# Row gathers held back by a written element, and x's sums loaded later, in both expert sweeps of an encoder layer

## The chip, the cores and the metric

One core of one Trainium2 chip runs the whole kernel. The metric is the device time of one execution in microseconds, as the median of several executions. Engines are called by their names: TensorE (PE in the profile, PEld for its weight loads), VectorE (DVE), ScalarE (ACT), GpSimd (POOL) and SyncE (SP), which issues the plain DMAs.

## The reference

One layer of an encoder, float32, 256 tokens (two blocks of 128, t = 0 and 1) of width 2048. Two kinds of attention, then an expert layer called PEER, then a last normalisation:

```python
x = x + mixed @ w_out[l]                                  # attention
x = x + peer_ffn(rms_norm(x, norm2_g[l]), ...)            # PEER, below
return rms_norm(x, final_norm_g)

q = (xt @ w_query).reshape(n_tok, PEER_HEADS, 2, 128)
scores = einsum('thcd,hcnd->thcn', q, sub_keys)           # 2 x 128 keys per head
...                                                       # top 16 of 16384 pairs per token and head
u = jnp.take(expert_u, eb, axis=0)                        # rows of the chosen experts
vv = jnp.take(expert_v, eb, axis=0)
act = jax.nn.gelu(jnp.einsum('td,thkd->thk', xb, u))
return jnp.einsum('thk,thkd->td', act * gb, vv)
```

Each token chooses 8 x 16 = 128 of 16384 experts. Per expert there is one row of 2048 numbers in u and one in v.

## The kernel before

The kernel does not gather whole rows of u and v. For most columns it computes with all 16384 experts on TensorE and picks the chosen values afterwards; only the last columns are gathered row by row. There are three stages after the attention.

**First sweep (u).** For columns 0 to 1535 of u, 192 units of 128 x 1024 numbers are loaded one after the other (SP issues the loads, `load_raw`, L158). `load_split` (L165) makes two rounded parts of each: hi on ScalarE (L169) and the remainder lo on VectorE (L170). TensorE multiplies hi (L792, eight matmuls) and lo (L794, eight) with the normalised tokens; a unit can't start before its hi, nor its second half before its lo. There are three buffers each for hi and lo. The sums land in the large array A (the arena), one slice of 512 columns for every two key rows, in order of the sweep; a slice is free for other use until its turn comes.

Beside it, VectorE does two other jobs, one piece at a time between the units' lo subtractions, in an order that a planner (`advance`, L687) writes out by hand: first the searches for the top 16 (they end in unit 52), then 256 dot products for columns 1536 to 2047 (`dot`, L648). Each dot product first has GpSimd gather 128 rows, one per token, by an indirect DMA (`gather`, L643), then VectorE multiplies and sums them (L650). VectorE's order is the program's order, since the sweep stands under `manual_schedule(engines={DVE})`; GpSimd's and SP's order is found by the compiler's scheduler. Where the gathered rows go is decided by a ring (`Slots`, L74): four buffers called wm, and, when the searches are done, the eight arena slices `PAIRS` = 52 to 59, which the searches used until then. One is added after every second unit (L811), and `add` puts it in front, so that it is the next that is handed out:

```python
if selected and opened and i % 2 == 0:
    p = opened.popleft()
    spares.add(arena[:, p * 512:(p + 1) * 512], 2 * p * KA // 8 - 4)
```

A gather into such a slice waits for the last reader that the search had there; it does not wait for VectorE to come to the line above.

**Extraction.** One-hot products pick the chosen activations out of A, apply the gelu and the gates and write the weights of all experts back into A. At its end the first three units of v are already loaded and multiplied in part (L948).

**Second sweep (v).** 192 units of v's columns 0 to 1471, two of 1024 and one of 896 columns in turn, go through `load_split` and twelve matmuls each (L931 hi, L932 lo, L933 hi) into six sums. Columns 1472 to 2047 are gathered: `weigh` (L1002) gathers 128 rows into one of five row buffers and VectorE adds them, weighted, to vsum (L1004). vsum starts as x's columns 1472 to 2047, loaded from DRAM (x2d) at L1000, ahead of the loop. The 256 weighs are spread evenly over the units by `spread` (L569), from unit `WEIGH` = 5 on; here too VectorE's order is the program's. The row buffers, vsum and two further load buffers (L998) lie in memory that the extraction's tiles give up when it ends. Before the change, the gathers for the first five weighs wait for nothing but that memory.

Of the kernel before, what the change touches and what calls it, by code (L numbers as in the profile page):

```python
# [9 lines left out]
F32 = mybir.dt.float32  # L10
# [8 lines left out]
P = 128  # L19
D = 2048  # L20
S = 256
NT = 2
# [14 lines left out]
V1 = 1472  # L37
VT = D - V1
# [23 lines left out]
EARLY_HI = (62, 63, 64)  # L62
EARLY_LO = (66, 68, 70)
EARLY_PE = (67, 68, 69, 70, 70, 70)
WEIGH = 5
LAST = 3
READY = 189
W_OUT_ORDER = (4, 5, 6, 7, 0, 1, 2, 3)
# [34 lines left out]
def encoder_layer_kernel(ctx: ExitStack, tc: tile.TileContext, x, gT, w_in, gq, gk, w_out, g2,  # L103
                         w_query, sub_keys, u_head, u_tail, v_head, v_tail, gf, cst, rope, bias_a, out):
    nc = tc.nc
# [9 lines left out]
    arena = A.rearrange("p a b c -> p (a b c)")  # L115
# [5 lines left out]
    def hTs(k, part, r):  # L121
        return hTa[:, k, part, r] if k < KA else hTb[:, k - KA, part, r]
# [8 lines left out]
    def take(n, at=None):  # L131
        if at is None:
            at = pos[0]
            pos[0] += n
        assert at + n <= NK * S, at + n
        return arena[:, at:at + n]

    def mm_bank(name="mm"):
        return psm.tile([P, 512], F32, name=name, tag="mm")

    def at_bank(name="at"):
        return psa.tile([P, 512], F32, name=name, tag="at")

    def small(n, name):
        return sm.tile([P, n], F32, name=name, tag=f"s{n}", bufs=8 if n < 8 else 4)
# [19 lines left out]
    def load_split(src):  # L165
        raw = loaded.popleft() if loaded else load_raw(src)
        hi, lo = (wp.tile([P, 1024], F32R, name=s, tag=s, bufs=3)[:, :raw.shape[-1]] for s in ("hi", "lo"))
        with tc.high_priority(AHEAD):
            nc.scalar.activation(hi, raw, AF.Copy)  # L169
            nc.vector.tensor_tensor(lo, raw, hi.bitcast(F32), op=OP.subtract)  # L170
        return hi, lo
# [13 lines left out]
    def ready_sqrt():  # L185

        tc.keep_in_program_order(nc.scalar.activation(small(1, "warm"), one, AF.Sqrt))
# [102 lines left out]
    rows = Ring([take(512) for _ in range(3)])  # L290
# [206 lines left out]
    x2d = dram.tile([P, NT * D], F32, name="x2d")  # L497
# [58 lines left out]
    bg = deque()  # L556
# [83 lines left out]

    spares = Ring([arena[:, i:i + DT] for i in range(SPARE * S, NK * S, DT)])

    def gather(rows_, table, t, j):  # L643
        nc.gpsimd.indirect_dma_start(out=rows_, out_offset=None, in_=table,  # L644
                                     in_offset=bass.IndirectOffsetOnAxis(ap=experts[:, j // 32, t * 32 + j % 32:t * 32 + j % 32 + 1], axis=0))
        return rows_
# [110 lines left out]
    rows, hots, hot, one_hots = {}, {}, {}, {}  # L757

    def rows_at(q):

        bc = wp.tile([P, 1024], F32, name="bc", tag="raw", bufs=RAW)
        nc.sync.dma_start(bc, bass.AP(tensor=i1d.tensor, offset=i1d.offset + 4 * q * P, ap=[[0, P], [1, 8 * P]]))
        rows[q // 2] = bc
# [13 lines left out]
    with query:  # L777
        for i in range(units):
            if i == SPARE * KA // 8 - 2:
                del raws[1]  # L780
            hi, lo = load_split(u_head[i])

            blocks = {}
            for b in range(8):
                e, k = divmod(8 * i + b, KA)
                blocks.setdefault(e, []).append((k, slice(b * P, (b + 1) * P)))
            for e, ks in blocks.items():
                if ks[0][0] == 0:
                    ps = mm_bank("act")
                for k, c in ks:  # L790
                    h = (hTa[:, k] if k < KA else hTb[:, k - KA]).rearrange("p a t -> p (a t)")
                    nc.tensor.matmul(ps, hi[:, c], h, start=k == 0, stop=False)  # L792
                for k, c in ks:
                    nc.tensor.matmul(ps[:, :S], lo[:, c], hTs(k, 0, slice(0, S)), start=False, stop=k == KA - 1)  # L794
                if ks[-1][0] == KA - 1:
                    ended.append((i + 3, A[:, e // 2, :, e % 2], ps))
                    with tc.high_priority(FIRST):
                        nc.scalar.activation(ended[-1][1], ps[:, :S], AF.Copy)
            while ended and (ended[0][0] <= i or i == units - 1):
                _, dst, sums = ended.popleft()  # L800
                nc.vector.tensor_tensor(dst, dst, sums[:, S:], op=OP.add)
            advance()
            if not searches and not selected:
                selected = True
                for t in range(NT):
                    select_transposed(t)
                opened = deque(range(*PAIRS))

            spares.now = i + 1
            if selected and opened and i % 2 == 0:  # L810
                p = opened.popleft()  # L811
                spares.add(arena[:, p * 512:(p + 1) * 512], 2 * p * KA // 8 - 4)
            if i == READY:
                tp = at_bank("parttp")
                for t in range(NT):
                    nc.tensor.transpose(tp[:, t * P:(t + 1) * P], part[:, t], ident)
                nc.scalar.activation(partT, tp[:, :S], AF.Copy)
                tp = at_bank("roottp")
                for t in range(NT):
                    nc.tensor.matmul(tp[:, t * P:(t + 1) * P], roots[:, NT + t:NT + t + 1].to_broadcast([P, P]), ident,  # L820
                                     start=True, stop=True)
                nc.scalar.activation(rootT, tp[:, :S], AF.Copy)
            if i == units - 1:
                for q in range(0, FULL, 2):
                    rows_at(q)
                for q in range(FULL):
                    hot_at(q)()
# [108 lines left out]
    def v_unit(i):  # L936
        return v_head[i][:, :2 * VW[2]] if i % 3 == 1 else v_head[i]
# [59 lines left out]
    vp = ctx.enter_context(tc.tile_pool(name="vp", bufs=2))  # L997
    raws.append((vp, MORE))  # L998
    vsum = vp.tile([P, NT, VT], F32, name="vsum", bufs=1)
    nc.sync.dma_start(vsum, x2d.rearrange("p (t d) -> p t d", t=NT)[:, :, V1:])  # L1000

    def weigh(t, j):  # L1002
        rows_ = gather(vp.tile([P, VT], F32, name="rows", bufs=5), v_tail, t, j)
        nc.vector.scalar_tensor_tensor(vsum[:, t], rows_, wN[:, t, j:j + 1], vsum[:, t], op0=OP.mult, op1=OP.add)  # L1004

    for t in range(NT):
        bg.extend((0.6, weigh, t, j) for j in range(P))


    ssl = [small(4, "ssl") for _ in range(NT)]  # L1010
# [1 line left out]
    with tc.manual_schedule(engines={DVE}):  # L1012
        for i in range(units):
            if i in halves:
                jobs = halves.pop(i)
                for job in jobs:
                    if job[2] == 0:
                        weights_at(job[1], slice(P, S))
            else:
                jobs = v_jobs(i, *load_split(v_unit(i)))  # L1020
                for job in jobs[::2]:
                    if job[2] == 0:
                        weights_at(job[1], slice(0, S))
            if i < units - LAST:
                for job in jobs:
                    v_matmuls(*job)
            else:
                last += jobs
            if i == 3 * units // 4:
                nc.sync.dma_start(xs[:, :, :V1], x2d.rearrange("p (t d) -> p t d", t=NT)[:, :, :V1])  # L1030
                load_gain(gf)
                ready_sqrt()
            if WEIGH <= i < units - 1:
                spread(units - 7 - i)
            if i == units - 5:
                for t in range(NT):
                    nc.vector.tensor_copy(xs[:, t, V1:], vsum[:, t])
                    square_sum(t, 3, ssl[t], v_chunk)
                    gained(t, 3)


        ends = ((2, 0, 1), (0, 1, 2))
        for t in range(NT):
            for c in ends[t]:
                for job in last:
                    if job[0] == t and job[2] == c:
                        v_matmuls(*job)
        for t in range(NT):
            for n, c in enumerate(ends[t]):
                xc = xs[:, t, v_chunk(c)]  # L1050
                nc.vector.tensor_tensor(xc, xc, v_bank(t, c), op=OP.add)
                with tc.high_priority(FIRST if t else 0):
                    square_sum(t, c, ssl[t], v_chunk)
                gained(t, c, nc.vector if t or n == VC - 1 else nc.gpsimd)
                if (t, n) == (1, 0):
                    scaled(0, ssl[0], ((3, nc.scalar), (1, nc.scalar), (0, nc.scalar), (2, nc.vector)))
        with tc.high_priority(FIRST):
            scaled(1, ssl[1], ((0, nc.vector), (1, nc.scalar), (2, nc.vector), (3, nc.scalar)))
# [78 lines left out]
```

## Time and profile before

| | |
|---|---|
| median of 3 runs | 1649.62 us (1647.13 to 1651.18) |
| profiled execution: its own time | 1659.56 us |
| profiled execution: span | 1657.8 us |
| mean granted TensorE clock | 0.994 |
| busy: TensorE, VectorE, ScalarE, GpSimd | 98%, 82%, 52%, 43% |
| first sweep in the trace | about 441 to 992 us |
| second sweep in the trace | from about 1131 us |

The span runs from the first to the last instruction of the profiled execution. Busy shares are averages over the span; engines work beside each other. The TensorE clock is granted at one of two levels, 1.00 (2.4 GHz) and 0.50 (1.2 GHz). "L792" is line 792 of the kernel; in a row, what stands before `<-` is written and what stands behind it is read, x8 is a count, and a bracket tells how long the engine had been idle and what ended that. "issue" in a bracket means that the engine waited for nothing that the profile shows.

### The profile page before, as it was taken

How to read it: one execution, taken by the hardware profiler on the slowest of the kernel's cores; microseconds unless marked ns; L12 is line 12 of the kernel's file. 1: busy time of each engine (PE TensorE's matmuls, PEld its weight loads, DVE VectorE, ACT ScalarE, POOL GpSimd, SP SyncE). 2: the span in 40 equal slices, each digit the busy share in tenths (PEclk: the TensorE clock that was granted, in tenths of full speed). 3: DMA queues.
4: the chain of work that ended last, by engine and by line, in shares of the span. 5: the costliest groups of instructions: out<-in, count | busy, mean ns of one | idle time of the engine just before them, and what ended most of it. 6: DMA issues, size and time to landing. Idle time of an engine off the chain costs nothing.

```text
span 1657.8 us, 25499 instructions
## 1 busy us (share of the span) xinstructions
PE 1627.9 (98%) x8706; PEld 1408.2 (85%) x8706; DVE 1358.7 (82%) x3030; ACT 867.1 (52%) x1255; POOL 705.2 (43%) x582
## 2 busy tenths in 40 slices
PE   8999999999999999999999999998999999999997
PEld 6888888888888878888888889997888888888886
DVE  6765465569799978888888859996899999999996
ACT  6565555454444444444444449995444444444444
POOL 0000000001233367676766613334676766667670
PEclk9999999999999999999999999999999999999999
DMA  7644554566777689999999863335999999999994
GB/s 248 198 144 153 166 202 165 191 206 202 231 253 245 235 303 345 347 340 338 347 341 313 300 241 116 128 118 201 356 389 365 347 357 344 356 349 359 340 365 146
DMA packets 126162, 443.04 MB, mean 267 GB/s; under 512 B 17744, under 2 KB 18640, under 8 KB 125648
## 3 DMA queue, kind: packets, MB, share of 16 engines
q1 hardware_dynamic: 85072, 298.78, 51.7%
q0 software_dynamic: 40960, 142.64, 24.3%
q8 instruction: 68, 1.11, 0.3%
q14 instruction: 62, 0.51, 0.1%
HBM read 437.02 MB, written 4.33 MB: 266 GB/s over the span
## 4 chain that ended last, share of the span: by engine, by line
PE 94%; DVE 2%; DMA 1%; ACT 1%; issue 1%; SPq 0%; ACTq 0%; DVEq 0%
PE act L792 21%; PE act L794 11%; PE o L932 10%; PE o L933 10%; PE o L931 10%; PE pr L275 7%; PE pr L276 7%; PE pr L274 7%; PE X L846 3%; PE W L896 3%; PE o1p L852 1%; PE sc L356 1%; PE po L387 1%; DMA raw<-in_v_head_dram 1%; DVE lo L170 1%
## 5 line engine op out<-in xcount | busy, mean ns | idle before, releaser
L169 ACT ACTIVATE hi<-raw 128x1024 fp32r<-128x1024 f32 (+1 forms) x445 | 464.8, 1045 | 529.9 <-PE o L933 241.0
L170 DVE TENSOR_TENSOR lo<-raw,hi 128x1024 fp32r<-128x1024 f32 (+1 forms) x445 | 536.0, 1205 | 187.2 <-ACT hi L169 166.0
L792 PE MATMUL act<-hTa,hi 128*128 128x512 f32 x1536 | 399.3, 395 | 0.8 <-issue 0.8
L644 POOL DMA_INDIRECT rows<-in_v_tail_dram,experts x256 | 321.1, 1254 | 161.7 <-DVE vsum L1004 96.0
L644 POOL DMA_INDIRECT A<-in_u_tail_dram,experts x128 | 158.5, 1239 | 471.9 <-DVE den L636 408.6
L792 PEld LDWEIGHTS act<-hTa,hi 128*128 128x128 f32 x1536 | 272.7, 190 | 46.9 <-issue 2.2
L931 PE MATMUL o<-hi,wt 128*128 128x512 f32 (+1 forms) x768 | 294.5, 384 | 3.9 <-ACT hi L169 3.9
L932 PE MATMUL o<-lo,wt 128*128 128x512 f32 (+1 forms) x768 | 294.3, 383 | 0.5 <-DVE lo L170 0.4
L933 PE MATMUL o<-hi,wt 128*128 128x512 f32 (+1 forms) x768 | 294.0, 383 | 0.0
L794 PEld LDWEIGHTS act<-hTa,lo 128*128 128x128 f32 x1536 | 219.5, 191 | 24.5 <-issue 3.5
L644 POOL DMA_INDIRECT wm<-in_u_tail_dram,experts x128 | 168.0, 1313 | 166.7 <-DVE wm L650 122.3
L794 PE MATMUL act<-hTa,lo 128*128 128x256 f32 x1536 | 226.5, 283 | 3.0 <-issue 3.0
L1004 DVE SCALAR_TENSOR_TENSOR vsum<-rows,h2t,vsum 128x576 f32<-128x576 f32 x256 | 208.7, 815 | 10.3 <-DMA rows<-in_v_tail_dram,experts 7.7
L931 PEld LDWEIGHTS o<-hi,wt 128*128 128x128 f32 x768 | 145.0, 189 | 28.5 <-ACT hi L169 4.3
L932 PEld LDWEIGHTS o<-lo,wt 128*128 128x128 f32 x768 | 144.9, 189 | 25.5 <-DVE lo L170 1.1
L933 PEld LDWEIGHTS o<-hi,wt 128*128 128x128 f32 x768 | 144.9, 189 | 24.6 <-DVE wt L926 0.6
L274 PE MATMUL pr<-hi,hTa 128*128 128x512 f32 x408 | 164.2, 404 | 0.0
L275 PE MATMUL pr<-lo,hTa 128*128 128x512 f32 x408 | 159.9, 392 | 0.3 <-DVE lo L170 0.2
L276 PE MATMUL pr<-hi,hTa 128*128 128x512 f32 x408 | 159.5, 391 | 0.0
L169 ACT ACTIVATE hi<-A 128x1024 fp32r<-128x1024 f32 x72 | 76.6, 1065 | 76.1 <-PE act L792 36.8
L170 DVE TENSOR_TENSOR lo<-A,hi 128x1024 fp32r<-128x1024 f32 x72 | 88.3, 1227 | 27.0 <-ACT hi L169 17.3
L889 POOL TENSOR_SCALAR o<-cs,I2T,h2t 128x128 f32<-128x128 f32 x64 | 54.9, 862 | 114.5 <-DVE h2t L880 56.2
(159 smaller groups left out, 2003.4 us busy)
## 6 DMA issues: line engine op xcount, KB each, us to landing
raw<-in_v_head_dram SPq DMA_DIRECT2D x128, 512.0 KB
raw<-in_u_head_dram SPq DMA_DIRECT2D x120, 512.0 KB
raw<-in_w_in_dram SPq DMA_DIRECT2D x72, 512.0 KB
A<-in_u_head_dram SPq DMA_DIRECT2D x72, 512.0 KB
raw<-in_v_head_dram SPq DMA_DIRECT2D x64, 448.0 KB
raw<-in_w_out_dram SPq DMA_DIRECT2D x32, 512.0 KB
raw<-in_w_query_dram SPq DMA_DIRECT2D x32, 512.0 KB
bc<-i1d SPq DMA_DIRECT2D x32, 512.0 KB
```

The lines of the kernel that those rows point to most:

```text
L169: nc.scalar.activation(hi, raw, AF.Copy)
L170: nc.vector.tensor_tensor(lo, raw, hi.bitcast(F32), op=OP.subtract)
L274: nc.tensor.matmul(ps[t], xT(k, 0, r), hi[:, c], start=first, stop=False)
L275: nc.tensor.matmul(ps[t], xT(k, 0, r), lo[:, c], start=False, stop=False)
L276: nc.tensor.matmul(ps[t], xT(k, 1, r), hi[:, c], start=False, stop=last)
L644: nc.gpsimd.indirect_dma_start(out=rows_, out_offset=None, in_=table, in_offset=bass.IndirectOffsetOnAxis(ap=experts[:, j // 32, t * 32 + ...
L792: nc.tensor.matmul(ps, hi[:, c], h, start=k == 0, stop=False)
L794: nc.tensor.matmul(ps[:, :S], lo[:, c], hTs(k, 0, slice(0, S)), start=False, stop=k == KA - 1)
L931: nc.tensor.matmul(ps, w[:, 0, r], hi[:, c], start=e == 0, stop=False)
L932: nc.tensor.matmul(ps, w[:, 0, r], lo[:, c], start=False, stop=False)
L933: nc.tensor.matmul(ps, w[:, 1, r], hi[:, c], start=False, stop=e == NK - 1)
L1004: nc.vector.scalar_tensor_tensor(vsum[:, t], rows_, wN[:, t, j:j + 1], vsum[:, t], op0=OP.mult, op1=OP.add)
```

## The change

A new helper writes one column of a row buffer on VectorE. A gather into that buffer writes the same place, so it has to wait until VectorE has reached the helper's instruction in its order. In the first sweep this is done for each of the eight arena slices as it is added to the ring. In the second sweep the gathers are now called from two places: five at unit `FETCH` = 4, each with its written element, and one after every weigh, for the weigh five later, without one. The first weigh moves from unit 5 to unit 7. The load of vsum moves from ahead of the loop to unit 4, behind the five gathers.

```diff
-WEIGH = 5
+FETCH, WEIGH, ROWS = 4, 7, 5
...
+    def held(rows_):
+
+        nc.vector.memset(rows_[:, 0:1], 0.0)
...
             if selected and opened and i % 2 == 0:
                 p = opened.popleft()
+                held(arena[:, p * 512:(p + 1) * 512])
                 spares.add(arena[:, p * 512:(p + 1) * 512], 2 * p * KA // 8 - 4)
...
     vsum = vp.tile([P, NT, VT], F32, name="vsum", bufs=1)
-    nc.sync.dma_start(vsum, x2d.rearrange("p (t d) -> p t d", t=NT)[:, :, V1:])
-
-    def weigh(t, j):
-        rows_ = gather(vp.tile([P, VT], F32, name="rows", bufs=5), v_tail, t, j)
+    picks, coming = deque((t, j) for t in range(NT) for j in range(P)), deque()
+
+    def fetch(hold=False):
+        if picks:
+            t, j = picks.popleft()
+            rows_ = vp.tile([P, VT], F32, name="rows", bufs=ROWS)
+            if hold:
+                held(rows_)
+            coming.append((t, j, gather(rows_, v_tail, t, j)))
+
+    def weigh():
+        t, j, rows_ = coming.popleft()
         nc.vector.scalar_tensor_tensor(vsum[:, t], rows_, wN[:, t, j:j + 1], vsum[:, t], op0=OP.mult, op1=OP.add)
-
-    for t in range(NT):
-        bg.extend((0.6, weigh, t, j) for j in range(P))
+        fetch()
+
+    bg.extend((0.6, weigh) for _ in range(NT * P))
...
+            if i == FETCH:
+                for _ in range(ROWS):
+                    fetch(hold=True)
+                nc.sync.dma_start(vsum, x2d.rearrange("p (t d) -> p t d", t=NT)[:, :, V1:])
             if WEIGH <= i < units - 1:
                 spread(units - 7 - i)
```

## Rows read from the trace of the kernel before

**Rows 1.** The page, part 1: busy time, share of the span, instructions.

```profile
PE 1627.9 (98%) x8706; PEld 1408.2 (85%) x8706; DVE 1358.7 (82%) x3030; ACT 867.1 (52%) x1255; POOL 705.2 (43%) x582
```

**Rows 2.** What TensorE waited for, whole span: us in total, times, longest.

```profile
PE o L931 <- ACT hi L169: 3.9, 1, 3.9
PE act L794 <- issue: 3.0, 5, 0.9
...
PE o L932 <- DVE lo L170: 0.4, 1, 0.4
```

**Rows 3.** Timeline of TensorE, units 53 to 59: start, us, what, count.

```profile
596.20 1.11 PE L794 MATMUL act<-hTa,lo 128*128 128x256 f32 x8
597.14 2.00 PE L792 MATMUL act<-hTa,hi 128*128 128x512 f32 x8
...
602.75 1.09 PE L792 MATMUL act<-hTa,hi 128*128 128x512 f32 x4
...
611.36 3.62 PE L792 MATMUL act<-hTa,hi 128*128 128x512 f32 x8
...
619.42 0.87 PE L792 MATMUL act<-hTa,hi 128*128 128x512 f32 x3
```

**Rows 4.** Stretches: us, busy PE, PEld, DVE, ACT, POOL, PEclk, DMA share, GB/s.

```profile
600.00:604.00 4.00, 3.84 (x21) 2.96 (x20) 1.40 (x5) 0.40 (x1) 3.08 (x4) 1.00 1.02 404
...
700.00:800.00 100.00, 100.00 (x573) 87.78 (x573) 86.50 (x177) 46.64 (x60) 71.53 (x59) 1.00 0.97 342
...
1149.60:1156.20 6.60, 6.17 (x15) 5.02 (x16) 5.08 (x6) 2.92 (x3) 1.69 (x1) 0.51 0.58 188
...
1300.00:1600.00 300.00, 300.00 (x1371) 257.13 (x1370) 275.74 (x315) 139.73 (x154) 201.60 (x163) 1.00 0.98 352
```

**Rows 5.** Timeline of GpSimd: the first and the last of 17 gathers in a row.

```profile
585.73 1.82 POOL L644 DMA_INDIRECT A<-in_u_tail_dram,experts  x1 [0.30 <-DVE A L626]
...
608.36 0.95 POOL L644 DMA_INDIRECT wm<-in_u_tail_dram,experts  x1 [0.30 <-issue]
```

**Rows 6.** Timeline of TensorE at the start of the second sweep.

```profile
1145.35 0.39 PE L933 MATMUL o<-hi,wt 128*128 128x512 f32 x1
1149.64 0.74 PE L931 MATMUL o<-hi,wt 128*128 128x448 f32 x1 [3.91 <-ACT hi L169]
...
1156.21 0.40 PE L931 MATMUL o<-hi,wt 128*128 128x512 f32 x1
```

**Rows 7.** The chain of waits there: start, us, what.

```profile
1137.81 10.75 DMA raw<-in_v_head_dram
```

**Rows 8.** Timeline there: SP's queue, and the first and last of five gathers.

```profile
1137.14 0.62 SPq L1000 DMA_DIRECT2D vsum<-x2d  x1
1137.42 1.04 POOL L644 DMA_INDIRECT rows<-in_v_tail_dram,experts  x1 [2.37 <-ACT A L897]
1137.81 1.06 SPq L160 DMA_DIRECT2D raw<-in_v_head_dram  x2
...
1142.53 1.43 POOL L644 DMA_INDIRECT rows<-in_v_tail_dram,experts  x1 [0.30 <-issue]
```

**Rows 9.** Timeline of VectorE: the one memset of a 128 x 1 column.

```profile
0.80 0.06 DVE L195 MEMSET one<- 128x1 f32 x1 [0.80 <-PEq L1125]
```

**Rows 10.** Timeline of VectorE in unit 53: lo, then a dot product on an arena row.

```profile
592.19 1.24 DVE L170 TENSOR_TENSOR lo<-raw,hi 128x1024 fp32r<-128x1024 f32 x1
...
593.69 0.68 DVE L650 SCALAR_TENSOR_TENSOR A<-A,h2t 128x512 f32<-128x512 f32 x1
```

**Rows 11.** Timelines late in the first sweep: two gathers, and the dot products that used them.

```profile
941.62 1.16 POOL L644 DMA_INDIRECT wm<-in_u_tail_dram,experts  x1 [0.39 <-DVE wm L650]
...
946.13 0.68 DVE L650 SCALAR_TENSOR_TENSOR wm<-wm,h2t 128x512 f32<-128x512 f32 x1
...
950.02 1.16 POOL L644 DMA_INDIRECT wm<-in_u_tail_dram,experts  x1 [0.39 <-DVE wm L650]
...
955.60 0.69 DVE L650 SCALAR_TENSOR_TENSOR wm<-wm,h2t 128x512 f32<-128x512 f32 x1 [1.01 <-DMA wm<-in_u_tail_dram,experts]
```

## The prediction

> **What bounds the kernel now.** I read the busy shares first, then what TensorE waited for, then the timeline around each wait. TensorE is busy for 98% of the span [rows 1], so a microsecond counts only if TensorE stops or slows for it. In the list of its waits two lie where the change works: 3.9 us for a rounded weight tile (hi, L169), with 0.4 us for its remainder (lo, L170), at the start of the second sweep, and several short waits at L794 for "issue", that is for nothing the profile shows, in the first sweep [rows 2].
>
> The first-sweep entry is larger than the list says. A unit of that sweep is eight L792 and eight L794 matmuls. Unit 54 starts at 597.14, unit 56 at 602.75, so a unit takes 2.80 us. Unit 57 starts only at 611.36 and unit 59 at 619.42 [rows 3]. From unit 56 to unit 59 pass 16.67 us where 3 x 2.80 = 8.40 are due: **8.3 us lost**. Units 57 and 58 take 8.06 us of it instead of 5.60, since TensorE is at half its clock: the eight L792 of unit 57 take 3.62 us, those of unit 54 took 2.00. That is 2.5 us; the other 5.8 are slow dispatch inside unit 56. Just before, the DMA engines are full, 404 GB/s at a share of 1.02 [rows 4], and GpSimd has issued 17 gathers in a row, the first at 585.73, the last at 608.36 [rows 5]. They are gathers into arena rows (A) that had come free, most of them for dot products that VectorE reaches much later.
>
> The second-sweep entry: the next matmul after 1145.35 was due 0.23 us later and starts at 1149.64, a hole of 4.1 us. The 15 matmuls from there to 1156.21, 6.57 us, run at a granted clock of 0.51; 0.39 us of that are the wait for lo, and half of the rest is lost to the clock: 3.5 us. Together **7.5 us** [rows 2, 4, 6]. The chain of waits names the cause: a weight load that took 10.75 us to land [rows 7]. On SP's queue it stands directly behind vsum, x's sums (576 KB), and beside five gathers that GpSimd issues from 1137.42 to 1142.53 [rows 8]. These gathers have no hurry: VectorE uses the first after unit 5.
>
> **The second sweep after the change.** The load of vsum moves on SP's queue behind the loads up to unit 4's, so unit 4's load goes out some 0.7 us earlier and has 576 KB less in front of it. The five gathers wait on VectorE for a written element behind unit 4's lo, some 1143.7 us instead of 1137.42. Waiting on GpSimd behind them: only further gathers of the same kind. Nothing holds up VectorE: the first weigh now stands in unit 7, three units or some 8 us behind the five memsets, while a gather takes about 5 us (below). Five memsets cost 5 x 0.06 us by the one memset in the trace [rows 9], beside TensorE. 256 weighs are spread from unit 7 on instead of unit 5, some 1% more VectorE work per unit; it is busy for 275.7 of 300 us there, so that is covered [rows 4]. Bounds: nothing gained, if loads still collide, to the whole 7.5. I take 7.5, because only the collision made the landing long. Next in line would be unit 5's load, behind vsum; it is needed 2.4 us later than unit 4's.
>
> **The first sweep after the change.** Here the same trick stands in another place. From the code, worked through by hand: when the searches end, in unit 52, every second unit opens one arena row, eight in all. The ring hands out the new row first, so the **next** dot product in VectorE's order takes it. VectorE's order is fixed by hand. In the trace of before, the place of the first memset is 592.19: there the lo of unit 53 begins, and at 593.69 the dot product on an A row follows [rows 10]. So between the memset and the instruction that needs the gather there lie 1.5 us of work at most. Before, the gather had been issued 8 us or more ahead; after, it can't start before the memset.
>
> What a gather takes, from its start on GpSimd until VectorE goes on, is seen where VectorE waited for one: start 950.02, use 955.60 after 1.01 us of waiting, so 5.6 us. Shorter ones exist: one that started at 941.62 was used, without a wait, at 946.13, so it took 4.5 us or less [rows 11]; the least that any row vouches for is the 0.95 us for which GpSimd is busy [rows 5]. I take 5.0, between the two, and 0.2 us for the way from VectorE to GpSimd. A hole is then 5.2 - 1.5 = 3.7 us, eight holes 29.6 us. What catches it: VectorE's idle time, 13.5 us in 100 [rows 4], over 16 units of 2.80 us makes 6.0 us; and its lead, lo of unit 53 ready at 593.43, used by TensorE at 596.20 [rows 3, 10], 2.8 us. The rest, 29.6 - 6.0 - 2.8 = **21 us**, stops TensorE, because lo comes late. At 4.5 us a gather it is 17 us. If the held gather also queues behind one other on GpSimd (17 in 22.6 us, so 1.4 us from one to the next [rows 5]), it is 32 us. Queued behind each held gather on GpSimd are the later gathers; if they come late, later dot products wait too, which the upper bound takes in. Eight memsets are 0.5 us of VectorE. Nothing later gives TensorE time back: it is the bound in every stage after.
>
> The 8.3 us of this stage go, since the 17 gathers no longer come at once. But whether the timed runs have them is a choice. The profiled execution took 1659.56 us, the median is 1649.62, 9.94 lower, and 8.3 of that would be this stall, in which TensorE waits for nothing that is named. I take it to be of the profiled execution alone. Sum against the profiled execution: 1659.56 + 21 - 7.5 - 8.3 = 1664.8; against the median: 1649.62 + 21 - 7.5 = **1663**.
>
> **The rivals.**
> 1. **The median holds the stall too.** The burst of gathers is in the program, so every run has it; against it speaks the gap of 9.94 us. Then 1663 - 8.3 = 1655.
>  The Trainium skill, "Runtime: NRT & Kernel Launch", in its part on the launch sequence, tells of a gap of about 6.2 us between a profile's total and the reported time, whatever the kernel. By that, 3.7 of the 9.94 us would be left for the stall, and an estimate for the median would lie between the two cases; no run here shows which.
> 2. **The holes are covered: faster.** Its place is VectorE between memset and dot product. It decides when a gather is ready within 1.5 + (6.0 + 2.8) / 8 = 2.6 us of its memset; then only the second sweep changes: 1649.62 - 7.5 = 1642, or 1634 if the stall goes as well. For it: VectorE runs well ahead of TensorE later in this sweep. Against it: the gather that was waited for took 5.6 us, and one of 2.4 us is in no row.
> 3. **A shorter gather.** In the trace a gather holds GpSimd for 0.95 us at 608.36 and for 1.82 us at 585.73 [rows 5]. If all eight are of the short kind, some 0.8 us each, 6 in all, come off: 1657.
>  The Trainium skill, "SBUF — State Buffer", "Who interferes with whom", says that a VectorE instruction with two SBUF inputs holds up a GpSimd instruction that reads SBUF. By that rule a VectorE standing in a hole would let the gather through faster; the trace has both lengths, and does not settle which one a held gather gets.
> 4. **Half clock on top.** TensorE, stopped every second unit, falls to 1.2 GHz, as it did behind both losses above [rows 3, 4]. The first of these spells cost 2.5 us; four of them make 1673.
>
> **How the numbers follow.** Chances: the forecast 0.42 (1663, by its bounds, 17 and 32 us, 1659 to 1674), rival 1 0.18, rival 2 0.20, rival 3 0.10, rival 4 0.10. A difference of 0.3%, 5 us, is about what a measurement of this kernel can tell from no change. Rival 1 lies at +5, so I split it between same and slower; of rival 2 nearly all is faster. Faster 0.19, same 0.11, slower 0.70. The range reaches from rival 2's 1642 to 1676, a little over rival 4, and leaves out rival 2 with the stall gone and a gather queued behind two others.
>
> **What the profile will show.** Right: TensorE without the 3.9 us wait at the start of the second sweep and with full clock there; vsum behind unit 4's load on SP's queue; eight waits of VectorE for a gather into A, 3 to 4 us each, and TensorE waiting for lo between units 53 and 69, about 21 us. Wrong: VectorE's waits there under 1.2 us, or TensorE busy through them (rival 2); a second sweep that still waits for a load; or the burst stall still there.

## The result, and the profile after

The changed kernel takes **1679.92 us** (median of 4 runs, 1678.66 to 1681.97); the kernel before took 1650.05 us in the same set (1647.13 to 1651.18). The ratio is 1.0181, with a 95% interval of 1.0169 to 1.0193: some 30 us slower. The forecast was 1663, with a range up to 1676. Its direction was right, its size too small by 17 us, and the result lies outside the range.

The page of the changed kernel: busy shares, the chain that ended last, and the dot products on arena rows (L654; L650 before).

```profile
PE 1634.3 (97%) x8706; PEld 1412.4 (84%) x8706; DVE 1357.2 (81%) x3043; ACT 867.1 (52%) x1255; POOL 711.8 (42%) x582
...
PE 81%; issue 7%; POOL 4%; DVE 3%; DMA 3%; ACT 1%; SPq 0%; POOLq 0%; ACTq 0%; DVEq 0%
...
L654 DVE SCALAR_TENSOR_TENSOR A<-A,h2t 128x512 f32<-128x512 f32 x128 | 85.7, 684 | 42.5 <-DMA A<-in_u_tail_dram,experts 42.5
```

The shares hardly moved against [rows 1]. The last row is the finding: VectorE stood 42.5 us ahead of dot products on arena rows, all of it for gathers. Asked for VectorE's waits between 590 and 690 us, the trace has one entry:

```profile
DVE A L654 <- DMA A<-in_u_tail_dram,experts: 42.5, 8, 5.9
```

Eight waits, one for each held row, the longest 5.9 us, and no other wait at all. So VectorE sets the pace from the first hole to the last. TensorE's own waits, over the whole span:

```profile
PE act L798 <- DVE lo L170: 21.4, 9, 3.8
...
PE o L937 <- DVE lo L170: 0.4, 1, 0.4
```

The 3.9 us for hi at the start of the second sweep [rows 2] are gone, a wait of 0.4 us for lo is still there, and 21.4 us of waiting for lo in the first sweep are new. That is less than the sweep lost. Unit 48 starts at 579.94 and unit 72 at 682.00; the stretch between them, first in the kernel after, then in an execution of the kernel before that had no stall (experiment 1); columns as in [rows 4]:

```profile
579.90:682.00 102.10, 80.71 (x393) 67.54 (x391) 59.54 (x133) 33.43 (x53) 50.44 (x43) 0.88 0.64 225
```

```profile
579.90:647.80 67.90, 67.90 (x393) 59.67 (x393) 61.94 (x129) 33.42 (x53) 52.61 (x41) 1.00 0.96 346
```

The same 24 units take 102.1 instead of 67.8 us: **34.3 us lost**. TensorE idles for 21.4 of them. For the other 12.9 it is busy, but slower, with a granted clock of 0.88 on average: it fell to 0.50 six times, each time in or just behind a wait for lo. VectorE's 59.54 us of work and 42.5 us of waiting make 102.0 of the 102.1 us, so nothing but its work and its holes set the length of this stretch. The DMA share falls from 0.96 to 0.64.

One of the holes, on VectorE:

```profile
592.26 1.22 DVE L170 TENSOR_TENSOR lo<-raw,hi 128x1024 fp32r<-128x1024 f32 x1
592.28 0.06 DVE L645 MEMSET A<- 128x1 f32 x1
593.40 0.41 DVE L805 TENSOR_TENSOR A<-A,act 128x256 f32<-128x256 f32 x1
598.72 0.69 DVE L654 SCALAR_TENSOR_TENSOR A<-A,h2t 128x512 f32<-128x512 f32 x1 [4.91 <-DMA A<-in_u_tail_dram,experts]
```

And on GpSimd, around the first hold (first two rows), the third (next two) and the sixth (last two):

```profile
591.99 1.15 POOL L648 DMA_INDIRECT wm<-in_u_tail_dram,experts  x1 [1.34 <-DVE wm L654]
593.45 0.94 POOL L648 DMA_INDIRECT A<-in_u_tail_dram,experts  x1 [0.31 <-issue]
...
611.84 1.67 POOL L648 DMA_INDIRECT wm<-in_u_tail_dram,experts  x1 [0.30 <-DVE A L645]
613.82 0.95 POOL L648 DMA_INDIRECT A<-in_u_tail_dram,experts  x1 [0.31 <-issue]
...
644.00 1.67 POOL L648 DMA_INDIRECT A<-in_u_tail_dram,experts  x1 [0.30 <-DVE A L645]
645.98 0.95 POOL L648 DMA_INDIRECT A<-in_u_tail_dram,experts  x1 [0.30 <-issue]
```

The element is written at 592.28. GpSimd is then busy with another gather, and starts the held one 1.17 us later. VectorE uses its row at 598.72, 5.27 us after that start. At the third hold another gather goes first once the element is written, and the held one starts 2.3 us behind it. The sixth to eighth hold are like the third; at the sixth (element at 643.66) the gather that goes first has an arena row too, one that a dot product had just freed. Which gather a waiting dot product waited for is told by the semaphore that both name in the trace. By it, in us:

| hold | 1 | 2 | 3 | 4 | 5 | 6 | 7 | 8 | mean |
|---|---|---|---|---|---|---|---|---|---|
| element to start of the held gather | 1.17 | 1.21 | 2.32 | 1.17 | 1.21 | 2.32 | 2.32 | 2.32 | 1.76 |
| start to use of the row | 5.27 | 5.22 | 4.64 | 6.28 | 6.24 | 3.78 | 4.04 | 4.62 | 5.01 |
| VectorE's wait ahead of that use | 4.91 | 4.89 | 5.76 | 5.92 | 5.91 | 4.91 | 4.83 | 5.41 | 5.32 |

All eight held gathers kept GpSimd for 0.94 or 0.95 us.

The second sweep, SP's queue and the first of the five gathers, which answer to [rows 8]; the load behind vsum, from the chain of waits; TensorE's wait for it; and the stretch of the first 15 units, columns as in [rows 4]:

```profile
1163.72 0.62 SPq L1049 DMA_DIRECT2D vsum<-x2d  x1
...
1171.12 1.04 POOL L648 DMA_INDIRECT rows<-in_v_tail_dram,experts  x1 [9.87 <-DVE rows L645]
...
1164.38 8.16 DMA raw<-in_v_head_dram
...
1174.94 0.50 PE L937 MATMUL o<-lo,wt 128*128 128x512 f32 x1 [0.39 <-DVE lo L170]
...
1157.20:1201.30 44.10, 43.62 (x209) 36.61 (x208) 34.14 (x51) 20.10 (x25) 25.75 (x20) 1.00 0.90 313
```

vsum now stands behind four weight loads instead of three, and the gathers start 13.9 us behind the sweep's first matmul (1157.24) instead of 6.4. The first 15 units, measured from that matmul to the first one of unit 15, take 44.02 us; before they took 50.89. The granted clock is 1.00 throughout. The 0.4 us for lo is not the wait of before: that stood in unit 4, this one in unit 5, whose load is now the one behind vsum and takes 8.16 us. That is the load which the prediction named as next in line. Outside these 15 units, the two kernels agree to 0.1 us from unit 72 of the first sweep on, and to 0.3 us ahead of unit 48.

### The profile page after: what moved, and what is told of

Read it like the earlier page. It is cut to its first block, busy times and chain, and to the rows that moved or that the text cites. A ratio compares the mean times of both kernels' runs of the same rounds, so it can differ in the third digit from the quotient of the medians.

```text
span 1677.1 us, 25522 instructions
## 1 busy us (share of the span) xinstructions
PE 1634.3 (97%) x8706; PEld 1412.4 (84%) x8706; DVE 1357.2 (81%) x3043; ACT 867.1 (52%) x1255; POOL 711.8 (42%) x582
## 4 chain that ended last, share of the span: by engine, by line
PE 81%; issue 7%; POOL 4%; DVE 3%; DMA 3%; ACT 1%; SPq 0%; POOLq 0%; ACTq 0%; DVEq 0%
PE act L796 14%; PE o L937 10%; PE o L938 10%; PE o L936 10%; PE act L798 7%; PE pr L275 7%; PE pr L276 7%; PE pr L274 7%; POOL wm L648 4%; PE X L851 3%; PE W L901 3%; DMA A<-in_u_tail_dram,experts 2%; DVE lo L170 1%; PE o1p L857 1%; PE sc L356 1%
## 5 line engine op out<-in xcount | busy, mean ns | idle before, releaser
L796 PE MATMUL act<-hTa,hi 128*128 128x512 f32 x1536 | 403.5, 399 | 0.0
L648 POOL DMA_INDIRECT rows<-in_v_tail_dram,experts x256 | 328.0, 1281 | 147.7 <-DVE vsum L1017 73.2
L796 PEld LDWEIGHTS act<-hTa,hi 128*128 128x128 f32 x1536 | 276.8, 192 | 46.2
L798 PEld LDWEIGHTS act<-hTa,lo 128*128 128x128 f32 x1536 | 221.0, 193 | 45.6 <-DVE lo L170 25.2
L798 PE MATMUL act<-hTa,lo 128*128 128x256 f32 x1536 | 228.6, 286 | 21.4 <-DVE lo L170 21.4
L654 DVE SCALAR_TENSOR_TENSOR A<-A,h2t 128x512 f32<-128x512 f32 x128 | 85.7, 684 | 42.5 <-DMA A<-in_u_tail_dram,experts 42.5
```

## The experiments

My theory behind the result: held gathers, issued just ahead of their use, stop VectorE (34 us lost), and the second sweep's part brings some 7 us. Its rivals: the excess over my 21 us is a queue on GpSimd, the half clock, or the 8.3 us stall that I had taken out. The runs came in three sets, the first and the third on the same chip, the second on another. The kernel before took 1657.18 us (1649.39 to 1660.41) in the first, which held experiments 2 to 5, 1650.44 (1645.98 to 1653.19) in the second (1, 6, 7 and 8), and 1649.89 (1645.77 to 1652.79) in the third (9, 10 and 11); ratios are to the runs of the kernel before in the same set. In the table, "units 48 to 72" and "first 15 units of v" are read from the timeline of TensorE, as above.

| kernel | first sweep | second sweep | units 48 to 72 | first 15 units of v | us | ratio |
|---|---|---|---|---|---|---|
| before, first profile | plain | before | 76.1 | 50.89 | | |
| after | 8 holds | after | 102.1 | 44.02 | 1679.92 | 1.0181 |
| 1. before again | plain | before | 67.8 | 47.69 | 1648.48 | one run |
| 2. second sweep only | plain | after | 76.0 | 44.55 | 1651.64 | 0.9967 |
| 3. first sweep only | 8 holds | before | 101.9 | 45.65 | 1685.44 | 1.0176 |
| 4. new row at the back | 8 holds, last in ring | after | 72.4 | 44.18 | 1651.71 | 0.9965 |
| 5. hold ahead of the dots | 8 holds, earlier | after | 93.5 | 43.74 | 1671.29 | 1.0088 |
| 6. half held | 4 holds | after | 85.1 | 43.90 | 1662.15 | one run |
| 7. no hold at all | plain | order alone | 67.9 | 48.36 | 1649.92 | 1.0000 |
| 8. every fourth unit | plain, fewer rows | after | 69.6 | 44.81 | 1647.76 | 0.9989 |
| 9. hold without the move | plain | 5 holds alone | 69.3 | 47.11 | 1648.38 | 0.9994 |
| 10. second sweep only, again | plain | after | 68.8 | 43.58 | 1645.83 | 0.9978 |
| 11. every fourth, again | plain, fewer rows | after | 70.0 | 44.65 | 1647.61 | 0.9987 |

**Experiment 1. The kernel before, profiled again.** No edit.

> The kernel before, unchanged, profiled once more. If both losses that I read from its first profile belong to the program, units 48 to 72 of the first sweep again take about 76.1 us instead of 67.8, with 'issue' waits in units 53 to 60, and the first 60 matmuls of the second sweep again take about 50.9 us with one wait of 3 us or more for hi. If they are chance, one or both are missing: about 67.8 us, about 44 to 46 us.

Measured: 48 to 72 in 67.8 us, TensorE without a single wait there; the second sweep's first 15 units in 47.69. So the stall of the first profile is not in every execution. The hole in the second sweep is there again, but smaller; TensorE's longest wait there:

```profile
PE o L931 <- ACT hi L169: 2.0, 1, 2.0
```

**Experiments 2 and 3. The two parts apart.** Experiment 2 is the changed kernel without the first sweep's hold, experiment 3 the kernel before with it:

```diff
# experiment 2, to the kernel after
-                held(arena[:, p * 512:(p + 1) * 512])
# experiment 3, to the kernel before (with the helper)
+                held(arena[:, p * 512:(p + 1) * 512])
```

> The changed kernel without the eight memsets of the first sweep; the second sweep stays changed. My theory (the eight holds of the first sweep cost some 34 us, the second sweep gains some 7): the holds gone, VectorE has no wait for a gather into A of over 3 us, TensorE's sum of waits for lo in the first sweep goes from 21.4 us to under 2, and the time is 1650 - 7 = 1643. Rival (the new calling order of the second sweep's gathers, or the changed order that the scheduler finds, costs most of the 30 us): 1660 or more. Second rival (the loss of the first sweep that the profile of before showed is in every execution of before): the time again 1643, but with slow dispatch of TensorE after unit 55 in this trace too.

> The kernel before with the eight memsets of the first sweep added, second sweep as before. My theory: the two halves add up, so 1650 + 34 = 1684, with eight waits of VectorE for a gather into A, 42 us in all, and the 3.9 us wait of TensorE at the start of the second sweep back. Rival (the second sweep did not gain, the 30 us are all of the first sweep): 1680.

Experiment 2: ratio 0.9967 [0.9947, 0.9987], a gain, but 1651.64 us instead of the 1643 expected. Its profile suggests why: the stall is back, and in that set the kernel before took 7 us more as well. TensorE's waits:

```profile
PE act L798 <- issue: 3.7, 4, 1.7
```

Experiment 3: ratio 1.0176 [1.0141, 1.0211], 1685.44 us. It repeats the first sweep of the change: VectorE's waits from 590 to 690 us are

```profile
DVE A L654 <- DMA A<-in_u_tail_dram,experts: 42.8, 8, 5.9
```

and units 48 to 72 take 101.9 us. So the loss is in the first sweep's eight holds. The ratio makes it 23 to 35 us, with the 34 inside; the 1685.44 us meet the 1684 expected, though the profiled execution took 1680.47 and the kernel before was 7 us above its usual time in this set. The other thing it shows I had not expected: with the second sweep untouched, its first 15 units took 45.65 us, not 50.89, and the wait for hi that was to come back was 0.6 us, not 3.9.

**Experiment 4. The held row at the back of the ring.** The holds stay; only their row is used last instead of first.

```diff
-                spares.add(arena[:, p * 512:(p + 1) * 512], 2 * p * KA // 8 - 4)
+                spares.views.append((arena[:, p * 512:(p + 1) * 512], 2 * p * KA // 8 - 4))
```

> The changed kernel, holds and all, but a new row goes to the back of the ring, so that at least four dot products (some 2.4 units, 6.8 us) lie between its memset and its use. My theory (what costs is the short way from memset to use, 1.5 us of work against a gather of 6.7 us): no wait of VectorE for A of over 2 us, time 1643 as without the holds. Rival (a hold costs in itself, since GpSimd stands still behind the held gather and the later gathers come late): waits of VectorE move to wm rows, time 1660 or more.

Ratio 0.9965 [0.9949, 0.9981], the same as without holds. VectorE's waits for gathers, 590 to 690 us:

```profile
DVE A L654 <- DMA A<-in_u_tail_dram,experts: 1.8, 2, 1.5
```

42.5 us of waiting became 1.8. **It is not the written element that costs, but that the very next dot product needs its row.** The 1651.71 us, where 1643 was expected, go with that set again; its profile has a shorter stall, 4.6 us in units 60 to 64.

**Experiment 5. The element written ahead of the unit's dot products**, which also opens the rows two units later.

```diff
+            if selected and opened and i % 2 == 0:
+                held(arena[:, opened[0] * 512:(opened[0] + 1) * 512])
+                held_now = True
+            else:
+                held_now = False
             advance()
...
-            if selected and opened and i % 2 == 0:
+            if held_now:
                 p = opened.popleft()
-                held(arena[:, p * 512:(p + 1) * 512])
```

> The changed kernel with each memset of the first sweep ahead of its unit's dot products instead of behind them (the eight rows open two units later, from unit 54 on). This puts one or two dot products, 0.6 us each, between memset and use, and the held gather comes ahead of the gathers that these dot products set free. If the excess over my forecast is the queue on GpSimd (memset to start of the gather 1.3 us instead of 0.2): the gap from memset to start falls to some 0.3 us, the holes to about 3.4 us, 27 us in all, and the time to 1665. If the queue stays: holes of about 4.4 us, 1672. If the half clock makes the excess: no less than 1675.

Ratio 1.0088 [1.0053, 1.0122], 1671.29 us. VectorE's waits:

```profile
DVE A L654 <- DMA A<-in_u_tail_dram,experts: 33.0, 8, 5.3
...
DVE lo L170 <- issue: 1.5, 2, 1.2
```

The holes shrink from 42.5 to 33.0 us, 4.1 each, and the lost time from 34.3 to 93.5 - 67.8 = 25.7 (the holes and the 1.5 us of "issue", less the 8.8 of idle time and lead). From element to use pass 6.5 us on average instead of 6.8, so 1.0 of the 1.2 us by which a hole is shorter is the added work. The queue did get shorter, but not to 0.3 us: element to start on GpSimd is 1.1 us on average instead of 1.76, and start to use 5.4 instead of 5.0. The time agrees with "the queue stays", but the rows open at other moments than in the change, so this run alone does not tell the queue from the gather's length. The times read from the change do that.

**Experiment 6. Every second row held.**

```diff
-                held(arena[:, p * 512:(p + 1) * 512])
+                if p % 2 == 0:
+                    held(arena[:, p * 512:(p + 1) * 512])
```

> The change with the held element at every second opened arena row only, four instead of eight. If each hold makes its hole of 5.3 us whatever the others do, and VectorE's idle time and lead (8.8 us) are spent once, units 48 to 72 take 67.8 + 4 x 5.3 - 8.8 = 80.2 us. If the loss is simply by the hold, half of the 34.3 us of the change, 84.9 us. If the unheld rows beside them bring back the burst of gathers, up to 8 us of 'issue' waits come on top.

Units 48 to 72 take 85.1 us, where the first theory gave 80.2 and the second 84.9. VectorE's waits, and GpSimd around the second hold (element written at 607.68):

```profile
DVE A L654 <- DMA A<-in_u_tail_dram,experts: 24.9, 4, 6.9
...
DVE lo L170 <- ACT hi L169: 2.3, 2, 1.2
```

```profile
608.02 1.68 POOL L648 DMA_INDIRECT wm<-in_u_tail_dram,experts  x1 [0.30 <-DVE A L645]
610.00 0.95 POOL L648 DMA_INDIRECT wm<-in_u_tail_dram,experts  x1 [0.30 <-issue]
611.25 0.94 POOL L648 DMA_INDIRECT A<-in_u_tail_dram,experts  x1 [0.30 <-issue]
```

The holes are longer, 24.9 / 4 = 6.2 us, and this one is the longest, 6.9: two other gathers went ahead of the held one, so it started 3.6 us behind its element. With the holes as measured, 24.9 - 8.8 = 16.1 against 17.3 us lost, "each hole, less idle time and lead once" fits within 1.2; "half of the eight" fits as well, 17.2. This run doesn't part the two. No "issue" waits of TensorE came on top. What it shows is that the holes grow beside unheld gathers: over the four, element to start is 2.1 us on average, against 1.76 with eight holds, and start to use 5.6 against 5.0.

**Experiment 7. No hold anywhere, the second sweep's new order alone.**

```diff
# to the kernel of experiment 2
-                    fetch(hold=True)
+                    fetch()
```

> No held element anywhere; in the second sweep only the order is new (gathers called at unit 4 without a written element, the first weigh in unit 7, the load of x's sums behind unit 4's load). If moving the load of x's sums is what freed unit 4's load, the first 60 matmuls of the second sweep take 44 to 45 us, as in the change, and the ratio to before is that of the kernel with the second sweep's part alone, 0.997. If the five gathers beside it are the cause, they start at about 1137 us again, a wait of 2 us or more for hi is left, the 60 matmuls take 48 to 51 us, and the ratio is 1.000.

Ratio 1.0000 [0.9988, 1.0011], 48.36 us for the first 15 units. TensorE's wait, the chain of waits with the weight load behind it, and the first of the five gathers:

```profile
PE o L935 <- ACT hi L169: 2.0, 1, 2.0
...
1131.06 10.91 DMA raw<-in_v_head_dram
...
1130.29 1.04 POOL L648 DMA_INDIRECT rows<-in_v_tail_dram,experts  x1 [2.37 <-ACT A L901]
```

Called later in the program, the gathers still start at the same point of the sweep, 6.4 us behind its first matmul: what starts them is their release, not their line. Beside them a weight load takes 10.91 us, as in [rows 7]. It is unit 5's this time, the one that now stands behind vsum; so moving vsum alone passes the wait on to the next unit and brings nothing.

**Experiment 9. The five gathers held, vsum loaded ahead of the loop as before.**

```diff
# to the kernel of experiment 2
     vsum = vp.tile([P, NT, VT], F32, name="vsum", bufs=1)
+    nc.sync.dma_start(vsum, x2d.rearrange("p (t d) -> p t d", t=NT)[:, :, V1:])
...
                     fetch(hold=True)
-                nc.sync.dma_start(vsum, x2d.rearrange("p (t d) -> p t d", t=NT)[:, :, V1:])
```

> No held element in the first sweep; in the second the five gathers are held at unit 4 as in the change, but the load of x's sums is back ahead of the loop, as before. If the five gathers alone delay the load of unit 4, the first 60 matmuls of the second sweep take 44 to 45 us, no wait for hi over 1 us is left, and the ratio to before is that of the second sweep's part alone in the same call. If the load of x's sums ahead of it counts as well, they take 46 us or more, with a wait for hi of 1 us or more, and the ratio lies between that one and 1.000.

Ratio 0.9994 [0.9985, 1.0003], 47.11 us. The wait for hi is half as long, and the weight load behind vsum takes 7.84 us without gathers beside it:

```profile
PE o L935 <- ACT hi L169: 1.0, 1, 1.0
...
1131.15 7.84 DMA raw<-in_v_head_dram
```

So neither half is enough: each alone leaves a wait of 1 to 2 us and a spell of half clock (mean granted clock 0.96 over the first 15 units in both). One profile each would not show that, since the second sweep of before took anything from 45.65 to 50.89 us; the times do. The ratio of experiment 7 is 1.0000, and this kernel took 1647.21 to 1653.01 us, where that of experiment 10, with both halves, took 1644.25 to 1647.51 in the same set. With both, the load behind vsum is unit 5's, which is needed later, and the gathers come too late to hold it up; the clock stays full. The stretch in the kernel of experiment 10:

```profile
1124.80:1168.40 43.60, 43.51 (x208) 36.59 (x207) 34.01 (x51) 20.23 (x25) 25.25 (x20) 1.00 0.91 319
```

**Experiments 8, 10 and 11. Which version is best.** Experiment 10 repeats experiment 2; 8 and 11 are the same kernel with rows opened after every fourth unit:

```diff
# experiments 8 and 11, to the kernel of experiment 2
-            if selected and opened and i % 2 == 0:
+            if selected and opened and i % 4 == 0:
```

> No held element in the first sweep; an arena row is opened after every fourth unit instead of every second; the second sweep as in the change. If the 'issue' stall comes from the long run of back-to-back gathers that the freed rows allow, it shrinks to under 3 us, units 48 to 72 take 68 to 71 us, and the ratio to before is 0.992 to 0.994. If the stall comes whenever the gathers start, it stays at 8 us and the ratio is 0.997. If fewer open rows let dot products wait, TensorE waits for lo at L798 and the ratio is over 0.997.

> The second sweep's part of the change alone, once more, against more runs of before. If that part is worth 4 us, as four profiles without held gathers (45.7 to 50.9 us for the first 60 matmuls) stand to those with them (43.7 to 44.8), the ratio is 0.9976. If it is worth the 7.5 us of my prediction, 0.9955. If the earlier 0.9967 was chance, 1.000.

> The second sweep's part with arena rows opened after every fourth unit, no held element in the first sweep, once more. If spreading the rows saves the chance of an 'issue' stall, it lies 1 to 6 us under the kernel with the second sweep's part alone in the same call; if that stall is rare on this chip, the two agree within 1 us, less the 1.8 us that one short wait for lo cost in its first profile.

Experiment 10: ratio **0.9978 [0.9969, 0.9987]**, 1645.83 us, 4 us under the kernel before, as the theory of 4 us had it. It beats both kernels. Every fourth unit gave 0.9989 [0.9977, 1.0001] and 0.9987 [0.9978, 0.9996], where 0.992 to 0.994 was one expectation; the latter is 1.8 us above experiment 10 in the same set. The profile of experiment 11 has two short waits of TensorE at L798 (0.59 and 1.02 us) in units 56 to 60, that of experiment 8 one of 1.5 us for lo. So fewer open rows save nothing where the stall is absent. Whether they would avoid it stays open, since none of the profiles of the second and third sets has one.

## Why the prediction was wrong in size

The mechanisms were right; two terms of the sum were mis-sized, the queue ahead of a held gather and the second sweep's gain.

**The hole per hold, the term that failed most.** I wrote: "A hole is then 5.2 - 1.5 = 3.7 us, eight holes 29.6 us." Measured: 42.5 / 8 = 5.3 us. Two of its three parts were right: "I take 5.0, between the two" was 5.0, and the work between was 1.76 + 5.01 - 5.32 = 1.45. The step that failed is "0.2 us for the way from VectorE to GpSimd", for which I gave no row. It was 1.76: at four holds GpSimd was busy with another gather when the element was written, at the other four one more went first. Eight times 1.56 is 12.5 of the 12.9 us missing. The idle time and lead that catch part of it, 8.8, measured 42.5 - 34.3 = 8.2. The case "If the held gather also queues behind one other on GpSimd ... it is 32 us" stood in the text as a bound. It was the likely case, and its 0.2 + 1.4 us are close to the 1.76: [rows 5] shows GpSimd issuing gathers back to back in just this stretch, so a new one finds a queue.

One sign came true by luck. I had TensorE "waiting for lo between units 53 and 69, about 21 us", and it waited 21.4. But my 21 us were to be the whole loss; the loss was 34.3, and the other 12.9 us went into a slower TensorE.

The length from start to use also answers rival 3. Its condition held, all eight held gathers were of the short kind, but its 6 us did not come off: the held gather at 593.45 took GpSimd only 0.94 us, and its row was used 5.27 us after the start. A short gather on GpSimd is not an early row. The Trainium skill, "Perfetto Trace Analysis", in its section "DMA Instruction — SWDGE (GPSIMD)", says that the profiled end there is the end of writing descriptors, not of moving data; the trace agrees. The Trainium skill, "DMA: Bandwidth & Descriptors", in its section "Anatomy of one DMA — SWDGE (gpsimd) path", gives 2.0 us plus the bytes at 436 GB/s, for these 128 x 512 floats an estimate of 2.6 us; the trace differs, with 3.8 to 6.3 us from start to use among the other transfers.

**The second sweep's gain.** I wrote "I take 7.5, because only the collision made the landing long." Against its own profile the change gained 50.89 - 44.02 = 6.9 us, so the cause was read rightly. But that profile was at the bad end: the three with this part of the kernel unchanged took 50.89, 47.69 and 45.65, mean 48.1, and the eight with the second sweep of the change 43.58 to 44.81, mean 44.2. The gain is **3.9 us** on average, and experiment 10's ratio says the same. The cause was the pair, gathers and vsum (experiments 7 and 9).

**The sum, mended.** 1650.05 + 34.3 - 3.9 = 1680.4; measured 1679.92. Of the 17 us between forecast and result, 13.3 are the first sweep's and 3.6 the second's.

**The stall.** "I take it to be of the profiled execution alone" held for the set that the forecast was about: an execution without it took 1648.48 us, beside a median of 1650.05. It is not a flaw of that one profile, though. In the first set of experiments it was in the profile of experiment 2, and shorter in that of experiment 4, and the kernel before took 7 us more there; that it was in those timed runs too fits, but they left no timeline. Rival 1 thus fell here, and could have held on another day. The gap of about 6.2 us that the Trainium skill, "Runtime: NRT & Kernel Launch", gives in its part on the launch sequence is one between a profile's total and the reported time. It had no bearing on the 9.94 us, which lie between two reported times, and no run here tests it: the span is not that total, and the reported time of experiment 1 is 1.8 us over its span, as that of the kernel after is (1678.85 and 1677.1).

**The rivals.** Rival 2 fell: VectorE's waits were 4.8 to 5.9 us each. Rival 4, half clock on top, happened and cost next to nothing: six spells, but with VectorE setting the pace (102.0 of the 102.1 us are its work and its holes), a slow TensorE only used up time in which it would have waited. The holes alone explain 42.5 - 8.8 = 33.7 of the 34.3 us. In the range, the bound of 32 us with the full gain of 7.5 gave 1674; the two mis-sized terms together went past it.

## What to carry to other kernels

A written element that holds back a gather is free where the row is used well behind it, and costs the gather's whole way, queue included, where the next instruction on that engine uses the row. Look at the order in which buffers are handed out: the same eight holds cost 34 us with the new row in front of the ring, and nothing that could be measured with it at the back. Price a gather from start to use, add the queue that its engine has at that moment (here 1.8 us on top of 5.0), and take a loss or a stall from more than one profile before it enters a sum.

## What was not expected of the hardware

The stall in the first sweep stops more than TensorE. From 600 to 613 us of experiment 2's profile, the waits of all engines:

```profile
DVE lo L170 <- issue: 6.1, 1, 6.1
ACT A L802 <- remote: 5.5, 1, 5.5
PEld act L798 <- issue: 5.2, 5, 2.0
PE act L798 <- issue: 3.7, 4, 1.7
...
DVE wm L654 <- issue: 2.4, 1, 2.4
```

TensorE and VectorE wait for nothing that the profile names, at the same time, and it costs 8 us. The stretch from 603.0 to 611.4 us, in experiment 2 and in experiment 1, which ran the same first sweep:

```profile
603.00:611.40 8.40, 3.73 (x15) 2.26 (x13) 2.35 (x6) 1.06 (x1) 4.87 (x5) 0.85 0.88 318
```

```profile
603.00:611.40 8.40, 8.40 (x50) 7.34 (x49) 8.32 (x18) 3.90 (x6) 6.88 (x6) 1.00 0.94 315
```

TensorE, VectorE and ScalarE do less than half of their work, while the transfers go on as usual, 318 against 315 GB/s. My prediction saw the run of 17 gathers as the cause (ten of them into arena rows, not all as it has it, and seven into wm). Experiment 1 speaks against that: there GpSimd issues gathers back to back from 586 to beyond 620 us, a longer run, beside the same traffic, and nothing stops. Nor is it the chip alone, since the first and the third set ran on the same one. What the stall is stays open.
